# Recurrence scores below 32 tokens on four 32-column TensorE tiles, in a compact tile; sample values and decode states on such tiles too

## The chip, the cores and the metric

One core of one Trainium2 chip. The metric is the device time of one execution in microseconds. The kernel before took 1286.46 us, the median of 3 runs (1283.77 to 1287.47).

## The reference, cut to what matters

One layer of a decoder trunk over 1024 prompt tokens and 8 samples of 8 tokens each (together 1088 columns in the kernel): RMSNorm, one input projection, three groups of heads on its result, an output projection, then a gated ConvFFN. The group that the change touches most is the gated linear recurrence (HGRN2), 4 heads, key and value width 128:

```python
def step(S, blk):
    qc, kc, vc, gc = blk
    A = jnp.cumsum(gc, axis=2)
    decay = jnp.exp(jnp.where(mask, A[:, :, :, None, :] - A[:, :, None, :, :], -jnp.inf))
    scores = jnp.einsum("bhtd,bhsd,bhtsd->bhts", qc, kc, decay)
    o = jnp.einsum("bhts,bhsv->bhtv", scores, vc) + jnp.einsum("bhtd,bhdv->bhtv", qc * jnp.exp(A), S)
    A_end = A[:, :, -1:, :]
    S = jnp.exp(A_end[:, :, 0, :])[..., None] * S + jnp.einsum("bhsd,bhsv->bhdv", kc * jnp.exp(A_end - A), vc)
    return S, o
```

So the score of token t on an earlier token s is a product over 128 features, each with the decay between s and t. The samples go through the same with a state that is handed in. The change also touches the cross-attention of the samples (softmax of scores times 256 memory values per sample).

## The kernel before, in words

Features lie on partitions, tokens along the free side. The large products are split in two: weights and activations each into a high and a low part (fp32r), three matmuls (lines 283 to 285) for each block of 128 x 128 weights. The products of the heads are plain f32; the trace shows each such matmul as two passes, and each pass as a weight load (PEld) and a matmul (PE).

`hgrn(h)` is a generator, one for each head, with 20 steps. The scores between tokens are made level by level. Level b (1, 2, 4, ..., 64) makes the scores of the pairs that lie in the two halves of one stretch of 2b tokens: K of the first half times Q of the second. Between levels VectorE scales K and Q in place by products of forget gates (`T`, lines 725 to 727), so that after level b the decay over 2b tokens is in them. Before the levels come the scores of a token on itself (`dg`, line 670, and `dgs` for the samples, line 674). The 1024 tokens are 8 blocks of 128, and `scT` holds for each block a 128 x 128 matrix of scores (s on partitions, t along the free side); `scS` is the same for the 64 sample columns.

For the diagonal and the levels up to 16 (line 701) each block is one matmul with all 128 columns of K as weights and 128 (diagonal) or 64 (levels) columns of Q moving, though only the small squares near the diagonal are wanted; VectorE copies these out of PSUM into `scT` under a mask (`copy_predicated`, lines 671 and 703; 675 and 720 for the samples). Levels 32 and 64 (line 710) use the K columns of one half only, 32 or 64 weight columns, placed on the tile of TensorE that belongs to the output partitions, and ScalarE copies the result (line 714). Samples have levels 1, 2 and 4 (`scs`, line 718).

After the levels, K is transposed, the states S of the 8 blocks are made one after another, and `o` is scores times V plus S times Q (lines 767, 769). For the samples `os` is one matmul of the scores (line 773) and then one for each sample with its own state of 128 x 128 as weights and 8 columns of Q moving (line 775). Three chunks of normalisation follow.

`xattn()` is the cross-attention. For the samples, `ssc` (line 588) makes the scores of four samples on four 32-column tiles of TensorE, and `so` (line 608) multiplies 128 x 128 values by 16 columns of probabilities.

`weave` sets the order: the steps of `hgrn` and `xattn` are spread among the steps of the input projection that still has to be done (`WIN`, units of three chunks of 362 or 364 columns), so that projection matmuls stand between one level and the next. A planner in the framework then places instructions on each engine by their readiness, so the order on TensorE is near the written one and not quite it. `with tc.high_priority()` puts the evacuation of the projection first.

`msk` holds the masks and is loaded as f32 and converted once. `chist` holds the samples' conv history (128 x 352 f32); it is loaded at the start on ScalarE's queue and first read in the up projection of the FFN (`start_a`, line 1180). `enter("ou", ...)` begins the output stage; `out_rows` (line 882) issues the loads of the residual rows `xb` on SP's queue there.

Of the kernel before, what the change touches and what calls it, by code (L numbers as in the profile page):

```python
# [50 lines left out]
def trunk(ctx, tc, I, O):  # L51
# [30 lines left out]
    def hrow(name, cols=512, p=128, dt=F32):  # L82
        return now["wk"].tile([p, cols], dt, tag="half", name=name, bufs=HB)
# [70 lines left out]
    cst = const.tile([128, NC], F32, name="cst")  # L154
    msk = const.tile([128, 5 * 64 + 128], U8, name="msk")
    poolw = const.tile([128, 2, 128], F32, name="poolw")
    chist = const.tile([128, FT, 8, 2], F32, name="chist")

    def load_consts():
        nc.sync.dma_start(out=cst, in_=I["cst"])  # L160
        yield
        mskf = hrow("mskf", 5 * 64 + 128)
# [408 lines left out]
    def xattn():  # L571
# [88 lines left out]
    MD = 5 * 64  # L660

    def hgrn(h):
        f, K, Q, V = FR[h], KR[h], QR[h], VR[h]

        dm = msk[:, MD:MD + 128]
        for half in range(2):
            ps = bank(f"dg{h}{half}", [128, 4, 128])
            for i in range(4):
                n = 4 * half + i
                mm(ps[:, i, :], K[:, n * 128:n * 128 + 128], Q[:, n * 128:n * 128 + 128], start=True, stop=True)  # L670
            nc.vector.copy_predicated(out=scT[:, 4 * half:4 * half + 4, :],
                                      mask=dm.unsqueeze(1).to_broadcast([128, 4, 128]), data=ps)
        ps = bank(f"dgs{h}", [64, 64])
        mm(ps, K[:, NP:NT], Q[:, NP:NT], start=True, stop=True)
        nc.vector.copy_predicated(out=scS, mask=msk[0:64, MD:MD + 64], data=ps)
        tt(out=Q[:, 0:NT], in0=Q[:, 0:NT], in1=f[:, 0:NT], op=ALU.mult)
# [16 lines left out]
        for li, b in enumerate(LEVELS):  # L693
            w = NT if b <= 4 else NP
            nb = w // (2 * b)
            Qo = Q[:, 0:NP].rearrange("p (n j two r) -> p n j two r", n=8, two=2, r=b)[:, :, :, 1, :]
            o4 = scT.rearrange("p n (j two r) -> p n j two r", two=2, r=b)[:, :, :, 1, :]
# [17 lines left out]
            if b <= 4:  # L715
                pss = bank(f"scs{h}_{b}", [64, 32 // b, b])
                q = Q[:, NP:NT].rearrange("p (j two r) -> p j two r", two=2, r=b)[:, :, 1, :]
                mm(pss, K[:, NP:NT], q, start=True, stop=True)
                o = scS.rearrange("p (j two r) -> p j two r", two=2, r=b)[:, :, 1, :]
                nc.vector.copy_predicated(out=o, mask=msk[0:64, li * 64:li * 64 + 32].rearrange("p (j r) -> p j r", r=b), data=pss)  # L720
            Tb = f[:, 0:w] if b == 1 else T[:, TO[b]:TO[b] + w // b]
# [143 lines left out]

    enter("ou", 8, NQ, 6)
    order = [2, 3, 4, 5, 6, 7, 0, 1]
    x1d = tc.dram_tile([128, 8, NT], F32, name="x1d")
# [686 lines left out]
def layout(inp):  # L1555
# [26 lines left out]
    A["cst"] = cst  # L1582
    msk = np.zeros((128, 5 * 64 + 128), np.float32)
    for li, b in enumerate(LEVELS[:5]):
        for j in range(64 // b):
            msk[2 * j * b:2 * j * b + b, li * 64 + j * b:li * 64 + j * b + b] = 1
    msk[:, 320:448] = np.eye(128)
    A["msk"] = msk
# [52 lines left out]
```

## Time and profile before

| | us |
|---|---|
| median of 3 runs | 1286.46 |
| lowest, highest | 1283.77, 1287.47 |
| the profiled execution, its own time | 1288.27 |
| span of its trace | 1286.5 |
| PE busy | 1246.2 |
| DVE busy | 941.5 |
| ACT busy | 537.1 |
| POOL busy | 259.8 |
| granted clock of TensorE, mean | 0.984 of full |

The span is what the trace covers; the execution's own time is 1.8 us more. The recurrence runs from about 78 to 350 us of the span, woven with the input projection; the rest of the cross-attention and the pooling mixer follow to about 440, then output projection, up projection and down projection. PE is TensorE's matmuls, PEld its weight loads, DVE VectorE, ACT ScalarE, POOL GpSimd.

### The profile page before, as it was taken

How to read it: one execution, taken by the hardware profiler on the slowest of the kernel's cores; microseconds unless marked ns; L12 is line 12 of the kernel's file. 1: busy time of each engine (PE TensorE's matmuls, PEld its weight loads, DVE VectorE, ACT ScalarE, POOL GpSimd, SP SyncE). 2: the span in 40 equal slices, each digit the busy share in tenths (PEclk: the TensorE clock that was granted, in tenths of full speed). 3: DMA queues.
4: the chain of work that ended last, by engine and by line, in shares of the span. 5: the costliest groups of instructions: out<-in, count | busy, mean ns of one | idle time of the engine just before them, and what ended most of it. 6: DMA issues, size and time to landing. Idle time of an engine off the chain costs nothing.

```text
span 1286.5 us, 23500 instructions
## 1 busy us (share of the span) xinstructions
PE 1246.2 (97%) x9348; PEld 1206.1 (94%) x9348; DVE 941.5 (73%) x1672; ACT 537.1 (42%) x1015; POOL 259.8 (20%) x294
## 2 busy tenths in 40 slices
PE   6999999999999899989999999999999989999996
PEld 6999899998987799989999999999999989999996
DVE  7775767658496645988887789788876967967633
ACT  7732414122245445655333333333433425644542
POOL 0000000000010000234444544454322000100142
PEclk9999999999999898989999999999999999999998
DMA  8131011122201445322434543454312578344333
GB/s 260 35 115 50 34 50 33 50 63 93 85 24 39 144 137 175 105 67 91 137 133 145 183 142 132 142 183 134 93 58 75 194 253 290 94 124 150 97 93 105
DMA packets 75822, 148.11 MB, mean 115 GB/s; under 512 B 9136, under 2 KB 31280, under 8 KB 75712
## 3 DMA queue, kind: packets, MB, share of 16 engines
q1 hardware_dynamic: 71920, 141.77, 33.9%
q0 software_dynamic: 1280, 4.34, 0.9%
q8 instruction: 73, 1.20, 0.4%
q10 hardware_dynamic: 2512, 0.50, 0.2%
q14 instruction: 37, 0.30, 0.1%
HBM read 110.66 MB, written 35.93 MB: 114 GB/s over the span
## 4 chain that ended last, share of the span: by engine, by line
PE 82%; DVE 9%; ACT 3%; issue 3%; DMA 2%; DVEq 0%; POOL 0%; SPq 0%; ACTq 0%; POOLq 0%
PE sc L701 3%; PE po L926 2%; PE po L925 2%; PE uUa L1165 2%; PE uUa L1163 2%; PE po L924 2%; PE uUa L1164 2%; PE pV L1311 2%; PE pV L1313 2%; PE pV L1312 2%; PE pU L1311 2%; PE pU L1313 2%; PE pU L1312 2%; PE uPa L1164 2%; PE uPa L1165 2%
## 5 line engine op out<-in xcount | busy, mean ns | idle before, releaser
L1299 DVE TENSOR_TENSOR dlp<-drp,dhp 128x512 fp32r<-128x512 f32 x81 | 56.8, 712 | 39.6 <-ACT dhp L1298 38.6
L1298 ACT ACTIVATE dhp<-drp 128x512 fp32r<-128x512 f32 x81 | 49.6, 625 | 76.5 <-PE pP L1312 22.3
L1283 DVE TENSOR_TENSOR xop<-B,xop 128x544 fp32r<-128x544 f32 x70 | 50.2, 732 | 13.1 <-ACT xop L1304 13.0
L1304 ACT ACTIVATE xop<-B 128x544 fp32r<-128x544 f32 x70 | 44.3, 650 | 26.9 <-DVE xop L1283 13.0
L1313 PE MATMUL pP<-xop,dlp 128*128 128x272 f32 x176 | 51.2, 292 | 4.4 <-DVE dlp L1299 4.4
L1312 PE MATMUL pP<-xop,dhp 128*128 128x272 f32 x176 | 51.3, 292 | 0.0
L1311 PE MATMUL pP<-xop,dhp 128*128 128x272 f32 x176 | 51.3, 292 | 0.0
L1311 PE MATMUL pU<-xop,dhp 128*128 128x272 f32 x176 | 50.7, 288 | 0.1
L1311 PE MATMUL pV<-xop,dhp 128*128 128x272 f32 x176 | 50.7, 288 | 0.0
L1312 PE MATMUL pU<-xop,dhp 128*128 128x272 f32 x176 | 50.6, 288 | 0.0
L1312 PE MATMUL pV<-xop,dhp 128*128 128x272 f32 x176 | 50.6, 288 | 0.0
L1313 PE MATMUL pU<-xop,dlp 128*128 128x272 f32 x176 | 50.6, 287 | 0.0
L1313 PE MATMUL pV<-xop,dlp 128*128 128x272 f32 x176 | 50.6, 287 | 0.0
L1126 DVE TENSOR_TENSOR g<-g,uc 128x272 f32<-128x272 f32 x66 | 46.3, 702 | 0.8
L1099 POOL TENSOR_TENSOR us0a<-ura 128x512 f32<-128x512 f32 x11 | 19.2, 1749 | 121.5 <-DMA ura<-in_wup 103.8
L1193 DVE SCALAR_TENSOR_TENSOR g<-a,vec,g 128x1104 f32<-128x1104 f32 x22 | 31.7, 1443 | 14.6 <-ACT g L1191 14.6
L1196 ACT ACTIVATE g<-g 128x1104 f32<-128x1104 f32 x22 | 24.8, 1129 | 40.6 <-DVE g L1195 40.6
L1195 DVE SCALAR_TENSOR_TENSOR g<-a,vec,g 128x1104 f32<-128x1104 f32 x22 | 39.7, 1803 | 0.0
L214 ACT ACTIVATE whi<-raw 128x1024 fp32r<-128x1024 f32 (+1 forms) x24 | 24.5, 1022 | 35.9 <-PE pq L284 17.1
L701 PEld LDWEIGHTS sc<-Q,K 128*128 128x128 f32 x320 | 37.9, 192 | 1.3 <-issue 0.9
L701 PE MATMUL sc<-Q,K 128*128 128x64 f32 x320 | 38.4, 272 | 0.0
L1313 PEld LDWEIGHTS pP<-xop,dlp 128*128 128x128 f32 x176 | 33.7, 192 | 4.6 <-DVE dlp L1299 4.6
(2292 smaller groups left out, 5113.1 us busy)
## 6 DMA issues: line engine op xcount, KB each, us to landing
ds<-in_wdown SPq DMA_DIRECT2D x44, 256.0 KB, 3.1
ura<-in_wup SPq DMA_DIRECT2D x22, 512.0 KB, 4.2
urb<-in_wup SPq DMA_DIRECT2D x22, 512.0 KB, 3.7
sd<-ds SPq DMA_DIRECT2D x44, 256.0 KB, 2.0
drp<-sd SPq DMA_DIRECT2D x44, 256.0 KB, 2.7
fd<-g SPq DMA_DIRECT2D x20, 544.0 KB, 4.2
B<-fd SPq DMA_DIRECT2D x40, 272.0 KB, 5.3
drp<-in_wdown SPq DMA_DIRECT2D x37, 256.0 KB, 3.3
```

What stands on the lines that cost most here:

```text
L701: mm(ps[:, n, :, :], K[:, n * 128:n * 128 + 128], Qo[:, n], start=True, stop=True)
L1126: tt(out=dst, in0=dst, in1=s_, op=ALU.mult)
L1164: mm(ps, wh[:, w], xl[:, k], start=False, stop=False, skip_group_check=True)
L1165: mm(ps, wl[:, w], xh[:, k], start=False, stop=k == 3, skip_group_check=True)
L1195: stt(out=cw[:, 0:1104], in0=aw[:, 0:1104], scalar=col(V_CW, 3 * f), in1=cw[:, 0:1104], op0=ALU.mult, op1=ALU.add)
L1283: tt(out=out, in0=in0, in1=in1, op=ALU.subtract)
L1298: act(out=wh, in_=raw, func=AF.Copy)
L1299: tt(out=wl, in0=raw, in1=wh.bitcast(F32), op=ALU.subtract)
L1304: act(out=t[:, 0], in_=x, func=AF.Copy)
L1311: mm(ps, w[0][:, c], h, start=start, stop=False, skip_group_check=True)
L1312: mm(ps, w[0][:, c], l, start=False, stop=False, skip_group_check=True)
L1313: mm(ps, w[1][:, c], h, start=False, stop=stop, skip_group_check=True)
```

## The change

The diagonal and the levels 1 to 16 of the scores go through a new helper, `blocks`: a block of 128 tokens is four matmuls, each with 32 columns of K as weights on its own 32-column tile of TensorE (`tile_position=(0, 32 * j)`) and with the columns of Q that belong to those 32 tokens moving: 32 for the diagonal, 16 for a level. The result of a block is compact, 128 x 32 or 128 x 16. The scores are kept in a compact tile `scC` (128 partitions, 8 blocks and the samples, 32 columns), which lies in the memory of `chist`. The masks shrink to 16 columns a level and 32 for the diagonal. After level 16 ScalarE copies the four 32 x 32 squares of each block from `scC` to their places in `scT`, and two for the samples to `scS`. The sample values (`so`) and the decode states (`os`) are split in the same way into four 32-column tiles, with 16 and 8 moving columns. The load of `chist` moves from the start (ScalarE's queue) to the beginning of the output stage (SP's queue).

```diff
-    msk = const.tile([128, 5 * 64 + 128], U8, name="msk")
+    msk = const.tile([128, 112], U8, name="msk")
...
-    nc.scalar.dma_start(out=chist, in_=I["chist"])
...
-                    mm(so[:, ft, b, :], v_[:, t, ft * 128:ft * 128 + 128], spT[:, b // 4, t, o:o + 16],
-                       start=t == 0, stop=t == 1)
+                    for c in range(0, 128, 32):
+                        mm(so[c:c + 32, ft, b, :], v_[:, t, ft * 128 + c:ft * 128 + c + 32], spT[:, b // 4, t, o:o + 16],
+                           start=t == 0, stop=t == 1, tile_position=(0, c))
...
+    scC = chist.rearrange("p f b l -> p (f b l)")[:, 0:288].rearrange("p (n c) -> p n c", n=9)
+    nc.gpsimd.memset(scC, 0.0)
...
+    def blocks(ps, K, Q, at, cols, n=4):
+
+        for j in range(n):
+            mm(ps[32 * j:32 * j + 32, 0:cols], K[:, at + 32 * j:at + 32 * j + 32], Q(j), start=True, stop=True,
+               tile_position=(0, 32 * j))
...
-        dm = msk[:, MD:MD + 128]
-        for half in range(2):
-            ps = bank(f"dg{h}{half}", [128, 4, 128])
-            for i in range(4):
-                n = 4 * half + i
-                mm(ps[:, i, :], K[:, n * 128:n * 128 + 128], Q[:, n * 128:n * 128 + 128], start=True, stop=True)
-            nc.vector.copy_predicated(out=scT[:, 4 * half:4 * half + 4, :],
-                                      mask=dm.unsqueeze(1).to_broadcast([128, 4, 128]), data=ps)
...
+        dm = msk[:, MD:MD + 32]
+        ps = bank(f"dg{h}", [128, 8, 32])
+        for n in range(8):
+            blocks(ps[:, n], K, lambda j: Q[:, n * 128 + 32 * j:n * 128 + 32 * j + 32], n * 128, 32)
+        nc.vector.copy_predicated(out=scC[:, 0:8], mask=dm.unsqueeze(1).to_broadcast([128, 8, 32]), data=ps)
+        ps = bank(f"dgs{h}", [64, 32])
+        blocks(ps, K, lambda j: Q[:, NP + 32 * j:NP + 32 * j + 32], NP, 32, 2)
+        nc.vector.copy_predicated(out=scC[0:64, 8], mask=dm[0:64], data=ps)
...
             if b <= 16:
-                ps = bank(f"sc{h}_{b}", [128, 8, 64 // b, b])
+                g = 16 // b
+                ps = bank(f"sc{h}_{b}", [128, 8, 16])
                 for n in range(8):
-                    mm(ps[:, n, :, :], K[:, n * 128:n * 128 + 128], Qo[:, n], start=True, stop=True)
-                m4 = msk[:, li * 64:li * 64 + 64].rearrange("p (j r) -> p j r", r=b).unsqueeze(1)
-                nc.vector.copy_predicated(out=o4, mask=m4.to_broadcast([128, 8, 64 // b, b]), data=ps)
+                    blocks(ps[:, n], K, lambda j: Qo[:, n, g * j:g * j + g], n * 128, 16)
+                m4 = msk[:, li * 16:li * 16 + 16].rearrange("p (j r) -> p j r", r=b)
+                o4 = scC.rearrange("p n (j two r) -> p n j two r", two=2, r=b)[:, :, :, 1, :]
+                nc.vector.copy_predicated(out=o4[:, 0:8], mask=m4.unsqueeze(1).to_broadcast([128, 8, g, b]),
+                                          data=ps.rearrange("p n (j r) -> p n j r", r=b))
...
             if b <= 4:
-                pss = bank(f"scs{h}_{b}", [64, 32 // b, b])
+                pss = bank(f"scs{h}_{b}", [64, 16])
                 q = Q[:, NP:NT].rearrange("p (j two r) -> p j two r", two=2, r=b)[:, :, 1, :]
...
+                blocks(pss, K, lambda j: q[:, g * j:g * j + g], NP, 16, 2)
+                nc.vector.copy_predicated(out=o4[0:64, 8], mask=m4[0:64], data=pss.rearrange("p (j r) -> p j r", r=b))
+            if b == 16:
+                for j in range(4):
+                    c = slice(32 * j, 32 * j + 32)
+                    act(out=scT[c, :, c], in_=scC[c, 0:8], func=AF.Copy)
+                    if j < 2:
+                        act(out=scS[c, c], in_=scC[c, 8], func=AF.Copy)
...
-            mm(ps[:, b, :], s0[b // 4][:, b % 4, :], Q[:, NP + 8 * b:NP + 8 * b + 8], start=False, stop=True,
-               skip_group_check=True)
+            for c in range(0, 128, 32):
+                mm(ps[c:c + 32, b, :], s0[b // 4][:, b % 4, c:c + 32], Q[:, NP + 8 * b:NP + 8 * b + 8],
+                   start=False, stop=True, skip_group_check=True, tile_position=(0, c))
...
     enter("ou", 8, NQ, 6)
+    nc.sync.dma_start(out=chist, in_=I["chist"])
```

The host builds the smaller masks to match.

## Rows read from the trace of the kernel before

**Rows 1.** The page: busy time of each engine with its share of the span and instructions; gigabytes a second in 40 slices of the span; the chain that ended last by engine.

```profile
PE 1246.2 (97%) x9348; PEld 1206.1 (94%) x9348; DVE 941.5 (73%) x1672; ACT 537.1 (42%) x1015; POOL 259.8 (20%) x294
...
GB/s 260 35 115 50 34 50 33 50 63 93 85 24 39 144 137 175 105 67 91 137 133 145 183 142 132 142 183 134 93 58 75 194 253 290 94 124 150 97 93 105
...
PE 82%; DVE 9%; ACT 3%; issue 3%; DMA 2%; DVEq 0%; POOL 0%; SPq 0%; ACTq 0%; POOLq 0%
```

**Rows 2.** Windows of the recurrence, about one for each head: length, then the busy time of PE, PEld, DVE, ACT and POOL with their instructions, the granted clock, the DMA share and GB/s.

```profile
78.60:141.00 62.40, 62.40 (x451) 59.33 (x450) 37.41 (x72) 15.41 (x30) 1.25 (x2) 0.97 0.17 54
141.00:214.00 73.00, 73.00 (x505) 66.49 (x504) 55.36 (x112) 26.73 (x53) 1.08 (x2) 1.00 0.13 44
214.00:290.00 76.00, 76.00 (x528) 71.79 (x527) 49.87 (x98) 17.16 (x32) 4.40 (x8) 0.98 0.18 57
290.00:350.00 60.00, 60.00 (x474) 55.23 (x472) 38.92 (x79) 15.29 (x30) 1.23 (x4) 1.00 0.28 91
```

**Rows 3.** Lines with shapes kept apart, TensorE's matmuls of the score levels: weight tile, moving shape, count, busy us and mean ns of one.

```profile
L701 PE MATMUL sc<-Q,K 128*128 128x64 f32 x320 | 38.4, 272 | 0.0
...
L710 PE MATMUL sc<-Q,K 128*32 128x32 f32 x128 | 2.8, 197 | 0.0
```

**Rows 4.** Timeline of TensorE's matmuls around level 8 of head 0, no sample scores: start us, length us, engine, line, operation, tiles, shape and count.

```profile
108.43 0.33 PE L284 MATMUL pi<-h3l,whi 128*128 128x362 f32 x1
...
108.76 0.33 PE L283 MATMUL pi<-h4h,whi 128*128 128x362 f32 x1
108.92 1.89 PE L701 MATMUL sc<-Q,K 128*128 128x64 f32 x16
...
110.87 0.33 PE L285 MATMUL pi<-h4h,wlo 128*128 128x362 f32 x1
```

**Rows 5.** The same around level 1 of head 0, with its sample scores.

```profile
87.92 0.33 PE L285 MATMUL pq<-h3h,wlo 128*128 128x362 f32 x1
88.08 1.90 PE L701 MATMUL sc<-Q,K 128*128 128x64 f32 x16
89.91 0.30 PE L718 MATMUL scs<-Q,K 128*64 128x32 f32 x2
...
90.41 0.33 PE L284 MATMUL pq<-h4l,whi 128*128 128x362 f32 x1
```

**Rows 6.** The same around the diagonal of head 3 (two sample passes follow the 16).

```profile
288.56 0.33 PE L285 MATMUL pg<-h3h,wlo 128*128 128x364 f32 x1
288.73 1.95 PE L670 MATMUL dg<-Q,K 128*128 128x128 f32 x16
...
291.13 0.33 PE L284 MATMUL pg<-h4l,whi 128*128 128x364 f32 x1
```

**Rows 7.** The same around the decode states of head 1.

```profile
196.20 1.95 PE L775 MATMUL os<-Q,s 128*128 128x8 f32 x16
198.00 0.41 PE L283 MATMUL pf<-h2h,whi 128*128 128x362 f32 x1
```

**Rows 8.** The same around the values of one sample.

```profile
334.26 0.33 PE L283 MATMUL pu<-h1h,whi 128*128 128x364 f32 x1
334.43 0.96 PE L608 MATMUL so<-spT,svt 128*128 128x16 f32 x8
...
335.49 0.33 PE L285 MATMUL pu<-h1h,wlo 128*128 128x364 f32 x1
```

**Rows 9.** The same around level 32 of head 0, which is on two 32-column tiles.

```profile
112.68 0.32 PE L284 MATMUL pi<-h0l,whi 128*128 128x362 f32 x1
112.94 0.70 PE L710 MATMUL sc<-Q,K 128*32 128x32 f32 x32
...
113.83 0.33 PE L283 MATMUL pi<-h1h,whi 128*128 128x362 f32 x1
```

**Rows 10.** Timeline of TensorE: the cross-attention scores of four samples (four tiles), of one (one tile) and of two (two tiles), 256 moving columns each.

```profile
292.39 1.09 PE L588 MATMUL ssc<-skt,qs 128*32 128x256 f32 x16
...
296.27 1.05 PE L588 MATMUL ssc<-skt,qs 128*32 128x256 f32 x4
...
301.59 1.06 PE L588 MATMUL ssc<-skt,qs 128*32 128x256 f32 x8
```

**Rows 11.** Windows (columns as in rows 2) just after the decode states of heads 0 and 2, and the timeline of the first half of those of head 3.

```profile
132.30:135.70 3.40, 3.40 (x13) 3.40 (x13) 0.69 (x1) 0.22 (x1) 0.00 (x0) 0.50 0.00 0
272.20:275.70 3.50, 3.50 (x13) 3.50 (x13) 1.17 (x2) 0.16 (x1) 0.00 (x0) 0.51 0.00 0
...
343.29 0.95 PE L775 MATMUL os<-Q,s 128*128 128x8 f32 x8
```

**Rows 12.** Lines with shapes kept apart, VectorE's copies under a mask: shape, count, busy us and mean ns of one, idle time before them.

```profile
L703 DVE COPY_PREDICATED scT<-msk,sc 128x512 f32<-128x512 uint8 x20 | 19.1, 956 | 25.3 <-PE sc L701 25.2
L671 DVE COPY_PREDICATED scT<-msk,dg 128x512 f32<-128x512 uint8 x8 | 5.9, 732 | 0.1
L720 DVE COPY_PREDICATED scS<-msk,scs 64x32 f32<-64x32 uint8 x12 | 2.7, 225 | 0.0
```

**Rows 13.** One window (columns as in rows 2) at the join of head 0 and head 1.

```profile
144.00:150.00 6.00, 6.00 (x29) 4.06 (x28) 6.00 (x14) 2.96 (x8) 0.00 (x0) 1.00 0.24 87
```

**Rows 14.** Lines with shapes kept apart, ScalarE's copies of level 32.

```profile
L714 ACT ACTIVATE scT<-sc 32x256 f32<-32x256 f32 x8 | 3.0, 374 | 49.7 <-PE sc L710 49.7
```

**Rows 15.** Timeline of ScalarE's DMA queue at the start.

```profile
1.67 0.45 ACTq L168 DMA_DIRECT2D chist<-in_chist  x1
```

More of the change, by code (lines that the diff above doesn't have):

```diff
@@ L161, in load_consts @@
         yield
-        mskf = hrow("mskf", 5 * 64 + 128)
+        mskf = hrow("mskf", 112)
         nc.sync.dma_start(out=mskf, in_=I["msk"])
@@ L657, in trunk @@
     nc.gpsimd.memset(scS, 0.0)
+    scC = chist.rearrange("p f b l -> p (f b l)")[:, 0:288].rearrange("p (n c) -> p n c", n=9)
+    nc.gpsimd.memset(scC, 0.0)
     sout = hrow("sout").rearrange("p (h v) -> p h v", h=4)
     TO = {2: 0, 4: 544, 8: 816, 16: 952, 32: 1016, 64: 1048, 128: 1064}
-    MD = 5 * 64
+    MD = 80
+    def blocks(ps, K, Q, at, cols, n=4):
+        for j in range(n):
+            mm(ps[32 * j:32 * j + 32, 0:cols], K[:, at + 32 * j:at + 32 * j + 32], Q(j), start=True, stop=True,
+               tile_position=(0, 32 * j))
     def hgrn(h):
         f, K, Q, V = FR[h], KR[h], QR[h], VR[h]
-        dm = msk[:, MD:MD + 128]
-        for half in range(2):
-            ps = bank(f"dg{h}{half}", [128, 4, 128])
-            for i in range(4):
-                n = 4 * half + i
-                mm(ps[:, i, :], K[:, n * 128:n * 128 + 128], Q[:, n * 128:n * 128 + 128], start=True, stop=True)
-            nc.vector.copy_predicated(out=scT[:, 4 * half:4 * half + 4, :],
-                                      mask=dm.unsqueeze(1).to_broadcast([128, 4, 128]), data=ps)
-        ps = bank(f"dgs{h}", [64, 64])
-        mm(ps, K[:, NP:NT], Q[:, NP:NT], start=True, stop=True)
-        nc.vector.copy_predicated(out=scS, mask=msk[0:64, MD:MD + 64], data=ps)
+        dm = msk[:, MD:MD + 32]
[6 more added lines that the diff above has]
+        nc.vector.copy_predicated(out=scC[0:64, 8], mask=dm[0:64], data=ps)
         tt(out=Q[:, 0:NT], in0=Q[:, 0:NT], in1=f[:, 0:NT], op=ALU.mult)
@@ L696, in hgrn @@
             Qo = Q[:, 0:NP].rearrange("p (n j two r) -> p n j two r", n=8, two=2, r=b)[:, :, :, 1, :]
-            o4 = scT.rearrange("p n (j two r) -> p n j two r", two=2, r=b)[:, :, :, 1, :]
             if b <= 16:
-                ps = bank(f"sc{h}_{b}", [128, 8, 64 // b, b])
+                g = 16 // b
+                ps = bank(f"sc{h}_{b}", [128, 8, 16])
                 for n in range(8):
-                    mm(ps[:, n, :, :], K[:, n * 128:n * 128 + 128], Qo[:, n], start=True, stop=True)
-                m4 = msk[:, li * 64:li * 64 + 64].rearrange("p (j r) -> p j r", r=b).unsqueeze(1)
-                nc.vector.copy_predicated(out=o4, mask=m4.to_broadcast([128, 8, 64 // b, b]), data=ps)
+                    blocks(ps[:, n], K, lambda j: Qo[:, n, g * j:g * j + g], n * 128, 16)
[3 more added lines that the diff above has]
+                                          data=ps.rearrange("p n (j r) -> p n j r", r=b))
             else:
@@ L715, in hgrn @@
             if b <= 4:
-                pss = bank(f"scs{h}_{b}", [64, 32 // b, b])
+                pss = bank(f"scs{h}_{b}", [64, 16])
                 q = Q[:, NP:NT].rearrange("p (j two r) -> p j two r", two=2, r=b)[:, :, 1, :]
-                mm(pss, K[:, NP:NT], q, start=True, stop=True)
-                o = scS.rearrange("p (j two r) -> p j two r", two=2, r=b)[:, :, 1, :]
-                nc.vector.copy_predicated(out=o, mask=msk[0:64, li * 64:li * 64 + 32].rearrange("p (j r) -> p j r", r=b), data=pss)
+                blocks(pss, K, lambda j: q[:, g * j:g * j + g], NP, 16, 2)
[6 more added lines that the diff above has]
+                        act(out=scS[c, c], in_=scC[c, 8], func=AF.Copy)
             Tb = f[:, 0:w] if b == 1 else T[:, TO[b]:TO[b] + w // b]
@@ L1582, in layout @@
     A["cst"] = cst
-    msk = np.zeros((128, 5 * 64 + 128), np.float32)
+    msk = np.zeros((128, 112), np.float32)
     for li, b in enumerate(LEVELS[:5]):
-        for j in range(64 // b):
-            msk[2 * j * b:2 * j * b + b, li * 64 + j * b:li * 64 + j * b + b] = 1
-    msk[:, 320:448] = np.eye(128)
+        for p in range(128):
+            if p % (2 * b) < b:
+                j = p % 32 // (2 * b)
+                msk[p, li * 16 + j * b:li * 16 + j * b + b] = 1
+    for p in range(128):
+        msk[p, 80 + p % 32] = 1
     A["msk"] = msk
```

## The prediction

> **What bounds the kernel now.** I read the page first: in the busy totals and the chain of waits the reader is to see that TensorE carries the end, busy 1246.2 of 1286.5 us and 82% of the chain, VectorE 9% [rows 1]. The change sits in the recurrence, so I then read that stage by windows. In 78.6 to 350 us TensorE is busy 100% of every window, VectorE 60 to 76%, ScalarE 23 to 37% [rows 2]. The lines view gives the price of what is replaced: the scores below 32 tokens are 320 passes and 38.4 us, about 120 ns a pass [rows 3]. (An f32 matmul stands in the trace as two passes, each with its own weight load: 8 blocks x 5 levels x 4 heads = 160 matmuls, 320 passes.) Last I read the timeline of single groups, since what counts is not an instruction's length but how long the projection's matmuls are held up.
>
> **How a group is priced.** Projection matmuls start 0.165 us apart (108.43 to 108.76, two steps) [rows 4]. A group between them costs the time from the start of the one before to the start of the second one after, less two steps (0.33). A level without sample scores: 110.87 - 108.76 - 0.33 = 1.78 us [rows 4]. A level with them: 90.41 - 87.92 - 0.33 = 2.16 [rows 5]. Diagonal with its sample part: 291.13 - 288.56 - 0.33 = 2.24 [rows 6]. The 16 passes of decode states: 198.00 - 196.20 = 1.80 [rows 7]. A sample's values: 335.49 - 334.26 - 0.33 = 0.90 [rows 8].
>
> These passes have 128, 64, 16 or 8 moving columns, yet all take 100 to 120 ns (38.4 us / 320 with 64 columns [rows 3], 1.80 / 16 with 8 [rows 7]). So the moving columns don't set the pace; the load of 128 weight columns does, as far as these rows tell. That load is what the change divides.
>
> **The new price.** The kernel already has such a group: the 32-token level runs 16 matmuls (32 passes) on two 32-column tiles, and costs 113.83 - 112.68 - 0.33 = 0.82 us, of which the burst is 0.50, from its first start to its last (0.70 [rows 9] less the 0.20 of the last pass [rows 3]); so 32 ns a pass on one tile (16 passes each), and about 0.32 us is for going into the narrow form and back. The new groups put 64 passes on four tiles, again 16 on each. Whether four tiles run as freely as two is shown by the sample scores of the cross-attention: 16 passes on four tiles last 1.09 us, 8 passes on two 1.06, 4 passes on one 1.05 [rows 10]. Tiles overlap almost wholly, so I price a new group by passes per tile: 0.82 us. Sample scores add one more short block on two tiles, 2 x 32 ns: 0.89.
>
> The Trainium skill ("TensorEngine Tiling (Array Packing)", Performance Considerations, Instruction Overhead) speaks against this: it gives each matmul some 60 cycles whatever its columns and advises against taking a tiling factor from a dimension that is already small, and here the moving side is 16 or 8. By that, if the cost is paid in one line, 64 passes at 25 ns (an estimate: 60 cycles at 2.4 GHz) are 1.6 us and the gain is gone; it is a rival below. The trace of before disagrees as far as it goes: 32 passes in 0.50 us are under 16 ns each [rows 9].
>
> **The change part by part, four heads.**
> Levels 1, 2, 4: 12 groups x (2.16 - 0.89) = 15.2 us.
> Levels 8, 16: 8 x (1.78 - 0.82) = 7.7.
> Diagonal: 4 x (2.24 - 0.89) = 5.4; with 32 moving columns it is the shape of [rows 9] itself.
> Decode states: the burst of 1.80 becomes 0.50 plus about 0.1 to load the next full weights plus 0.1 to go into the narrow form = 0.7; 4 x 1.1 = 4.3.
> Sample values: 8 groups, 8 passes per tile: 0.32 + 0.25 = 0.57 for 0.90; 8 x 0.33 = 2.6.
> Together 35.2 us off TensorE, all on the path in a stage where TensorE never rests.
>
> Clock: twice, after the decode states of heads 0 and 2, the granted clock falls to 0.50 for 3.4 us [rows 11], the 1.2 GHz level. TensorE had just run 16 passes of 8 moving columns. Head 3, whose 16 passes stand in two halves of 0.95 us, has no fall behind the first [rows 11], and the new burst is shorter than such a half. I take both falls as gone: half of 3.4, twice = 3.2 (own bounds: 0 gained, or as many new ones lost).
>
> VectorE: 28 predicated copies of 512 columns (19.1 + 5.9 = 25 us) become 4 of 256 and 20 of 128. Unseen in that form; between 0.22 us (the 64x32 copy) and 0.73 (the 512) [rows 12], nearer the small one for 128: about 0.27, and 0.4 for 256. That is 25 - 5.4 - 1.6 = 18 us less, 4.5 a head, beside TensorE. It matters at the joins between heads, where VectorE is busy 6 of 6 us [rows 13]: there TensorE saves 1.35 on the diagonal and VectorE only 2 x 0.73 - 0.4 = 1.06 ahead of the product of Q. I give back 0.3 x 3 joins, 1 us.
>
> ScalarE gets six copies a head from the compact tile into scT and scS, at most 6 x 0.37 = 2.2 us by the 32x256 copy [rows 14]. Their reader, the `o` matmuls, stands two levels later, so they cost nothing by themselves; what is queued behind them is the evacuation of the next projection (sigmoid, then VectorE, then the bank). Cover is ScalarE's idle two thirds. Bounds 0 to 8.8 us; I take 1.
>
> DMA: the load of chist leaves ScalarE's queue at 1.67 us [rows 15] and goes to SP's queue at the output stage, ahead of the four xb loads and the weights behind them. It waits for the last ScalarE copy of head 3, which is out of the way a stage earlier, and its reader is in the FFN. One more issue of 0.45 us: nothing, or 0.45 if exposed. At the start 176 KB less is moved, and the mask is smaller: between 0 and 0.7 us (176 KB at the 260 GB/s of that slice [rows 1]); I take 0, as TensorE's start hangs on ScalarE too. The memset of the compact tile is on GpSimd, which is nearly idle [rows 2].
>
> Sum: 35.2 + 3.2 - 1 - 1 = 36.4. The profiled execution took 1288.27 us, 1.8 above the median of the runs, so 1251.9 there and 1250.1 against the median.
>
> **The rivals.**
> (a) Four tiles don't run as freely as two. That they do is seen for passes of 256 columns [rows 10]; for short ones the 0.50 us of level 32 [rows 9] may be an issue pace, 32 passes at 16 ns, and not the tiles'. Then 64 passes take 1.0: groups cost 1.33 and 1.39, savings are 12 x 0.77 + 8 x 0.45 + 4 x 0.85 + 4 x 0.6 + 8 x 0.08 = 19, and the time is 1250 + 16 = 1266. Chance 0.12. For it: the same number fits both readings. Against: four tiles end within the time of one [rows 10].
> (b) VectorE's chain becomes the bound: each level's scores must be copied and K and Q scaled before the next level. TensorE then gets back only what VectorE saves, 18 us: 1286.5 - 18 = 1268. For it: 6 of 6 us at the joins [rows 13]. Against: 60 to 76% in the stages as a whole [rows 2], and the chain per level shortens by the copy. Chance 0.12.
> (c) Slower: passes on different tiles stand in one line. Place: every new group; price 32 ns a pass (the pace of one tile [rows 9]): 64 passes are 2.0 us, groups 2.34 and 2.47, so +0.56 x 8, +0.31 x 12, +0.23 x 4, states +0.43 x 4, sample values +0.43 x 8 = +14, time 1301. It decides from about 25 ns a pass, where a group (64 x 0.025 + 0.32 = 1.9) costs what it costs now. Against: the overlap of tiles [rows 9, 10]. Chance 0.06.
> (d) The line at a lower price, at break-even: no change, 1284 to 1288. Chance 0.04. By the skill's 25 ns the estimate is 1286.
>
> **How the numbers follow.** Forecast 0.66, own range 1243 to 1259 (clock falls -3 to +3, ScalarE up to 8.8, start 0.7, unseen copies). The range is widened upward to 1269 to take in (a) and (b); what is left out is (c), (d) and the ends. Downward 1242. A measurement of this kernel tells about 0.3%, 4 us. Faster by more than that: 0.66 + 0.12 + 0.12 = 0.90; within: 0.04; slower: 0.06.
>
> **What would show it.** In the changed profile: score passes four times as many, bursts of 0.5 us for 64 passes with projection matmuls held up 0.8 to 0.9 us; 1.3 would be (a), over 2 would be (c). TensorE's idle time before score groups stays under 1 us a head; if it grows and is put down to VectorE, (b). No fall of the clock behind the decode states, and none new behind scores. The evacuations' waits on ScalarE unchanged. Stages after 430 us as long as before. I am wrong if short passes on four tiles don't overlap, or if the time taken off TensorE comes back as waits.

## The result, and the profile after

The changed kernel takes 1245.51 us, the median of 4 runs (1240.97 to 1246.40), against 1286.97 (1283.77 to 1289.69) for the kernel before beside it: a ratio of 0.9672 [0.9639, 0.9705]. That is 41.5 us less where 36.4 were forecast; the forecast of 1250.1 is 4.6 us above the median and the range held it. From profiled execution to profiled execution it is 1288.27 to 1246.40, 41.9 us.

The page of the changed kernel, busy totals and chain by engine, beside [rows 1]:

```profile
PE 1204.8 (97%) x10916; PEld 1161.0 (93%) x10916; DVE 927.3 (75%) x1668; ACT 545.1 (44%) x1039; POOL 259.3 (21%) x295
...
PE 82%; DVE 11%; issue 3%; ACT 3%; DMA 2%; SPq 0%; DVEq 0%; POOL 0%; ACTq 0%; POOLq 0%
```

TensorE still carries the end with the same share of the chain, and is busy 41.4 us less, nearly the whole of what the kernel gained. So what came off TensorE came off the end, and nothing new stands in its place.

The first product of the output projection tells in which part of the kernel that was. The view of one tile, `po`, first for the kernel after:

```profile
L940 PE MATMUL po<-c,ow000h x8: 286/410/428, 399.5 to 404.1; 128*128 128x272 f32 x8
```

and for the kernel before:

```profile
L924 PE MATMUL po<-c,ow000h x8: 288/428/593, 441.2 to 446.5; 128*128 128x272 f32 x8
```

The output projection starts at 399.5 instead of 441.2 us, 41.7 earlier; the same view of the down projection's `pP` gives 989.7 instead of 1031.0. All of the gain lies ahead of the output stage, where the change was made. From there to the end the kernel takes 845.1 us, and took 845.2 before.

Lines with shapes kept apart of the kernel after, TensorE's score levels, then VectorE's masked copies; columns as in [rows 3] and [rows 12]:

```profile
L669 PE MATMUL sc<-Q,K 128*32 128x16 f32 x1280 | 14.8, 185 | 0.0
...
L711 DVE COPY_PREDICATED chist<-msk,sc 128x128 f32<-128x128 uint8 x20 | 7.1, 354 | 5.4 <-PE sc L669 3.0 <-PE scs L669 1.9
...
L679 DVE COPY_PREDICATED chist<-msk,dg 128x256 f32<-128x256 uint8 x4 | 1.8, 442 | 0.4 <-PE dgs L669 0.4
```

1280 passes take 14.8 us of TensorE, where 320 took 38.4 [rows 3]. One pass is still 185 ns long, against 272: the gain is not in a shorter pass but in how many are under way at once. The masked copies of the recurrence's prompt tokens take 7.1 + 1.8 = 8.9 us, for 25.0 [rows 12], 16 less for the 18 forecast.

What counts is how long the projection is held up, so the groups are read on the timeline of TensorE's matmuls (columns as in [rows 4]): level 1 of head 0 with its sample scores, level 8 of head 0, the diagonal of head 1, the decode states of head 1, those of head 3 and what follows them, and the values of one sample, all of the kernel after:

```profile
86.22 0.33 PE L284 MATMUL pq<-h3h,wlo 128*128 128x362 f32 x1
86.47 0.71 PE L669 MATMUL sc<-Q,K 128*32 128x16 f32 x62
...
87.01 0.19 PE L669 MATMUL scs<-Q,K 128*32 128x16 f32 x1
...
87.03 0.18 PE L669 MATMUL sc<-Q,K 128*32 128x16 f32 x1
...
87.45 0.33 PE L283 MATMUL pq<-h4l,whi 128*128 128x362 f32 x1
...
95.24 0.33 PE L283 MATMUL pi<-h0l,whi 128*128 128x364 f32 x1
95.50 0.74 PE L669 MATMUL sc<-Q,K 128*32 128x16 f32 x64
...
96.44 0.33 PE L282 MATMUL pi<-h1h,whi 128*128 128x364 f32 x1
...
138.52 0.73 PE L669 MATMUL dg<-Q,K 128*32 128x32 f32 x62
...
139.52 0.33 PE L284 MATMUL pq<-h0h,wlo 128*128 128x362 f32 x1
...
178.59 0.72 PE L790 MATMUL os<-Q,s 128*32 128x8 f32 x64
179.24 0.43 PE L282 MATMUL pf<-h2h,whi 128*128 128x362 f32 x1
...
302.89 0.32 PE L790 MATMUL os<-Q,s 128*32 128x8 f32 x17
...
304.16 0.88 PE L801 MATMUL oss<-osq,cst 128*128 128x364 f32 x2
304.97 0.45 PE L608 MATMUL so<-spT,svt 128*32 128x16 f32 x32
...
305.61 0.33 PE L282 MATMUL pg<-h5h,whi 128*128 128x362 f32 x1
```

By the rule of the prediction (start to start of the second one after, less 0.33) level 8 costs 96.44 - 95.24 - 0.33 = 0.87 us for 1.78 [rows 4], level 1 87.45 - 86.22 - 0.33 = 0.90 for 2.16 [rows 5]. The states hold up the next matmul 179.24 - 178.59 = 0.65 us for 1.80 [rows 7]. The diagonal and the values here don't stand behind a projection matmul, so I add the way in that level 8 shows, 95.50 - 95.24 = 0.26: the diagonal is 0.26 + 1.00 (138.52 to 139.52) - 0.33 = 0.93 for 2.24 [rows 6], a sample's values 0.26 + 0.64 (304.97 to 305.61) - 0.33 = 0.57 for 0.90 [rows 8]. The states of head 3 run as one burst with the values of two samples, 302.89 to 304.16, with one way in and out; that is 1.27 us where 0.65 + 2 x 0.57 would be 1.79.

Windows of the kernel after, columns as in [rows 2]: one for each head, the join of heads 0 and 1 ahead of them, and one in the down projection that an experiment needs:

```profile
137.00:143.00 6.00, 6.00 (x97) 4.57 (x96) 6.00 (x14) 2.65 (x6) 1.08 (x2) 1.00 0.12 45
...
77.50:132.00 54.50, 54.50 (x808) 50.88 (x808) 35.16 (x74) 18.65 (x38) 1.25 (x2) 1.00 0.19 63
132.00:188.00 56.00, 56.00 (x806) 50.59 (x805) 42.73 (x92) 23.21 (x49) 1.08 (x2) 1.00 0.14 49
188.00:254.00 66.00, 66.00 (x869) 61.06 (x869) 45.79 (x97) 20.76 (x43) 3.13 (x5) 1.00 0.18 61
254.00:306.00 52.00, 51.99 (x1024) 43.17 (x1023) 40.44 (x90) 18.23 (x41) 2.51 (x7) 1.00 0.38 117
...
990.00:1000.00 10.00, 5.53 (x34) 5.32 (x33) 9.16 (x16) 3.45 (x7) 0.55 (x1) 0.83 0.64 220
```

TensorE is busy all of the time in each head, VectorE now up to 78% (40.44 of 52), and the granted clock is full throughout: the two falls of [rows 11] are gone. At the join VectorE is busy 6 of 6 us as before [rows 13], and TensorE as well.

### The profile page after: what moved, and what is told of

It reads as the page before. It is cut to its first block, busy times and chain, and to the rows that moved or that the text cites. A ratio compares the mean times of both kernels' runs of the same rounds, so it can differ in the third digit from the quotient of the medians.

```text
span 1244.6 us, 26679 instructions
## 1 busy us (share of the span) xinstructions
PE 1204.8 (97%) x10916; PEld 1161.0 (93%) x10916; DVE 927.3 (75%) x1668; ACT 545.1 (44%) x1039; POOL 259.3 (21%) x295
## 3 DMA queue, kind: packets, MB, share of 16 engines
q0 software_dynamic: 1280, 4.34, 0.9%
## 4 chain that ended last, share of the span: by engine, by line
PE 82%; DVE 11%; issue 3%; ACT 3%; DMA 2%; SPq 0%; DVEq 0%; POOL 0%; ACTq 0%; POOLq 0%
PE po L942 2%; PE po L941 2%; PE uUa L1181 2%; PE po L940 2%; PE uUa L1179 2%; PE uUa L1180 2%; PE pV L1327 2%; PE pV L1328 2%; PE pV L1329 2%; PE pU L1327 2%; PE pU L1328 2%; PE pU L1329 2%; PE uPa L1180 2%; PE uPa L1181 2%; PE uPa L1179 2%
## 5 line engine op out<-in xcount | busy, mean ns | idle before, releaser
L1212 ACT ACTIVATE g<-g 128x1104 f32<-128x1104 f32 x22 | 24.8, 1129 | 41.9 <-DVE g L1211 41.9
L1215 DVE TENSOR_TENSOR g<-g,ra 128x560 f32<-128x560 f32 x22 | 36.9, 1678 | 0.0
L1328 PEld LDWEIGHTS pP<-xop,dhp 128*128 128x128 f32 x176 | 33.7, 191 | 0.0
```

The lines of the kernel that those rows point to most:

```text
L1328: mm(ps, w[0][:, c], l, start=False, stop=False, skip_group_check=True)
```

## The experiments

**Theory A**, that of the prediction: a group is priced by the passes on its busiest 32-column tile, some 32 ns each, because passes on different tiles overlap; the time saved lies on the end because TensorE never rests there. **Theory B**: the gain comes from VectorE's smaller copies. **Theory C**: a pace of issue, or of the whole array, sets the price, and the widths don't matter. The kernels ran in three groups, each beside the kernel before: order of the tiles, 64-column tiles and more moving columns beside 1291.29 us; sample parts undone, more and less work for VectorE and level 64 beside 1289.56; the sample parts alone, two and four blocks and chist at both places beside 1287.85. Sums are held against the 1245.51 of the changed kernel, which was measured in a group of its own.

**Order of the tiles.** The same 64 passes, first all blocks on tile 0, then on tile 1, and so on:

```diff
-                for n in range(8):
-                    blocks(ps[:, n], K, lambda j: Qo[:, n, g * j:g * j + g], n * 128, 16)
+                for j in range(4):
+                    c = slice(32 * j, 32 * j + 32)
+                    for n in range(8):
+                        mm(ps[c, n], K[:, n * 128 + 32 * j:n * 128 + 32 * j + 32], Qo[:, n, g * j:g * j + g],
+                           start=True, stop=True, tile_position=(0, 32 * j))
```

Expected:

> Same matmuls for the levels 1 to 16, but all eight blocks of one 32-column tile stand in the program before the next tile's. Theory A (tiles work side by side only where the queue holds matmuls of several tiles close together): 64 passes at 32 ns go nearly in one line, a level group costs about 2.3 us in place of 0.88, 20 groups make +20 to +30 us, time 1266 to 1276 us. Theory B (a group costs its passes per tile, whatever the order): 1245.5 us, groups still 0.88. Everything else is as in the changed kernel.

Measured: 1269.32 us, ratio 0.9822 [0.9768, 0.9876]. The timeline of TensorE around level 8 of head 0:

```profile
99.75 0.33 PE L283 MATMUL pi<-h0l,whi 128*128 128x364 f32 x1
100.01 1.90 PE L710 MATMUL sc<-Q,K 128*32 128x16 f32 x64
...
102.11 0.33 PE L282 MATMUL pi<-h1h,whi 128*128 128x364 f32 x1
```

The group costs 102.11 - 99.75 - 0.33 = 2.03 us for 0.87. 20 groups x 1.16 = 23.2 more than 1245.51 is 1268.7, and 1269.32 was measured. This is rival (c) brought about by order alone: with the tiles one after another the narrow form of a level without sample scores costs more than the full one (1.78 [rows 4]). Count, widths and work of the passes are unchanged, so a fixed price per pass (theory C) falls.

**64-column tiles.** Two tiles of 64 instead of four of 32, so half the passes and half of the scores left out (of each 64 columns of K one half meets the wrong Q):

```diff
-                    blocks(ps[:, n], K, lambda j: Qo[:, n, g * j:g * j + g], n * 128, 16)
+                    for j in range(2):
+                        c = slice(64 * j, 64 * j + 64)
+                        mm(ps[c, n], K[:, n * 128 + 64 * j:n * 128 + 64 * j + 64], Qo[:, n, 2 * g * j:2 * g * j + g],
+                           start=True, stop=True, tile_position=(0, 64 * j))
```

Expected:

> Levels 1 to 16 as two matmuls of 64 weight columns a block in place of four of 32, 16 columns moving, so half the passes, each with twice the weight columns. The Q columns of the second 32 tokens of each pair are left out, so these scores are not the reference's; VectorE's copies are unchanged. Theory A (a pass lasts as long as the load of its weight columns, tiles side by side): 16 passes of 61 ns on each of two tiles, burst 0.98 us, group 1.3, +8.5 us, time 1254. Theory B (the number of passes counts, a line at some 9 ns a pass as the changed kernel's 64 in 0.55 us would also allow): burst 0.28, group 0.6, time 1240.

Measured: 1254.91 us, ratio 0.9716 [0.9652, 0.978]. The timeline as above:

```profile
96.38 0.33 PE L283 MATMUL pi<-h0l,whi 128*128 128x364 f32 x1
96.64 1.11 PE L710 MATMUL sc<-Q,K 128*64 128x16 f32 x32
...
97.96 0.33 PE L282 MATMUL pi<-h1h,whi 128*128 128x364 f32 x1
```

Half as many passes cost more: 97.96 - 96.38 - 0.33 = 1.25 us, 0.38 more. Level 1 of head 0, whose sample scores stay on 32-column tiles, costs 87.56 - 85.81 - 0.33 = 1.42, 0.52 more. 8 x 0.38 + 12 x 0.52 = 9.3, and 9.4 was measured. The weight columns set the price, not the number of passes; rival (a), a pace of 16 ns a pass whatever the tile, would have made this group shorter.

**More moving columns, 32 and 64.** All 32 tokens of a tile move instead of the 16 wanted, or 64 (where the copy takes the first 32, so every second tile's scores are those of other tokens). The edit of the matmuls, without that of the copy:

```diff
-                    blocks(ps[:, n], K, lambda j: Qo[:, n, g * j:g * j + g], n * 128, 16)
+                    blocks(ps[:, n], K, lambda j: Q[:, n * 128 + 32 * j:n * 128 + 32 * j + 32], n * 128, 32)
```

and for 64 columns

```diff
+                    blocks(ps[:, n], K, lambda j: Q[:, n * 128 + 64 * (j // 2):n * 128 + 64 * (j // 2) + 64], n * 128, 64)
```

Expected, for 32 and then for 64:

> Levels 1 to 16 with all 32 columns of Q of a tile moving in place of the 16 that are wanted; the copy takes the wanted half. Theory A (weight load sets the pace up to 32 moving columns, as for the diagonal): groups 0.88 to 0.92, time within 1 us of 1245.5. Theory B (moving columns set the pace): burst 0.55 becomes 1.1, +0.55 x 20 = +11 us, time 1256.

> Levels 1 to 16 with 64 columns of Q moving on each tile (the 64 around it); the copy takes the first 32 of them, so for every second tile the scores are of other tokens than the reference's. Theory A (the longer of weight load and moving columns, tiles side by side): 64 columns of f32 last about 54 ns a pass (61 ns a pass at level 64, which has both 64), 16 a tile, burst 0.87 to 0.98, group 1.2 to 1.3, +6.5 to +8.5 us, time 1252 to 1254. Theory B (a pass costs the same whatever moves): 1246.

Measured with 32: 1245.30 us, ratio 0.9636 [0.9582, 0.969]; with 64: 1251.18, ratio 0.968 [0.9627, 0.9733]. The timeline of level 8 with 32 columns:

```profile
95.70 0.76 PE L669 MATMUL sc<-Q,K 128*32 128x32 f32 x64
```

and with 64:

```profile
95.32 0.32 PE L284 MATMUL pq<-h7h,wlo 128*128 128x362 f32 x1
95.57 1.10 PE L669 MATMUL sc<-Q,K 128*32 128x64 f32 x64
...
96.87 0.33 PE L283 MATMUL pi<-h0l,whi 128*128 128x364 f32 x1
```

Twice the columns are nearly free: bursts of 0.76 for 0.74 us, and no difference in time. Four times the columns cost 96.87 - 95.32 - 0.33 = 1.22 us a group, 0.35 more (20 x 0.35 = 7.0, and 5.7 was measured): 0.35 / 16 passes on a tile = 22 ns a pass, from 32 to some 54. That fits a pass that lasts as long as the longer of its weight load and its moving columns: up to 32 columns the load of 32 weight columns, at 64 the moving ones.

**Sample parts undone.** Sample values and decode states as one full-width matmul again, the scores as changed:

```diff
-                    for c in range(0, 128, 32):
-                        mm(so[c:c + 32, ft, b, :], v_[:, t, ft * 128 + c:ft * 128 + c + 32], spT[:, b // 4, t, o:o + 16],
-                           start=t == 0, stop=t == 1, tile_position=(0, c))
+                    mm(so[:, ft, b, :], v_[:, t, ft * 128:ft * 128 + 128], spT[:, b // 4, t, o:o + 16],
+                       start=t == 0, stop=t == 1)
...
-            for c in range(0, 128, 32):
-                mm(ps[c:c + 32, b, :], s0[b // 4][:, b % 4, c:c + 32], Q[:, NP + 8 * b:NP + 8 * b + 8],
-                   start=False, stop=True, skip_group_check=True, tile_position=(0, c))
+            mm(ps[:, b, :], s0[b // 4][:, b % 4, :], Q[:, NP + 8 * b:NP + 8 * b + 8], start=False, stop=True,
+               skip_group_check=True)
```

Expected:

> The changed kernel with decode states and sample values back on the full 128 columns. Theory A (they are worth their TensorE time, and the clock fell because of the decode states): +4.3 (states) + 2.6 to 3.6 (values), and the two falls of the clock behind the states of some heads come back, up to +3.2: time 1252 to 1256. Theory B (the falls went for another reason): no fall to 0.5 between 100 and 350 us, time 1252.

Measured: 1262.78 us, ratio 0.9794 [0.9762, 0.9825], 17.3 above the changed kernel and more than expected. Windows just behind the decode states of heads 1 and 2, and over the sample values:

```profile
181.20:184.60 3.40, 3.40 (x13) 3.40 (x13) 0.69 (x1) 0.22 (x1) 0.00 (x0) 0.50 0.00 0
249.50:252.90 3.40, 3.40 (x12) 3.40 (x13) 1.23 (x2) 0.22 (x1) 0.00 (x0) 0.50 0.00 0
...
314.30:324.50 10.20, 10.20 (x42) 10.20 (x42) 3.89 (x7) 3.34 (x8) 0.00 (x0) 0.50 0.18 52
```

The falls of the clock to 1.2 GHz are back, and longer: 3.4 + 3.4 + 10.2 = 17.0 us at half, which costs 8.5. The groups' own price is 4 x 1.15 (states) + 8 x 0.33 (values) = 7.2; together 15.7 of the 17.3; from the first diagonal to the last projection matmul the two traces differ by 15.6. Ahead of each fall TensorE had run the 16 full-width passes with 8 moving columns; here the values of the samples, 8 full-width passes with 16 columns each, follow those of head 3 closely, and the fall lasts over them.

**The sample parts alone**, added to the kernel before (the same edit the other way round). Expected:

> The kernel before with sample values and decode states alone on 32-column tiles, scores as before. Theory A: -4.5 (states) -3.7 (values), and the two falls of the clock behind the states gone, -3.2: time 1275. Theory B (the falls come from something else in the stage, such as the full-width scores): falls to 0.5 between 100 and 350 us stay, time 1278.

Measured: 1277.22 us, ratio 0.9909 [0.988, 0.9939], 10.6 less than the kernel before beside it. One window over its recurrence:

```profile
79.00:340.00 261.00, 260.99 (x2337) 240.74 (x2335) 181.51 (x357) 74.54 (x145) 7.96 (x16) 1.00 0.19 63
```

The clock is full throughout, with the score groups still as before. So the falls go with the states and values and not with the scores; 7.2 for the groups and 3.4 for the two falls [rows 11] make 10.6.

**More work for VectorE.** A copy of 512 columns under a mask of zeros after each level, which changes no score:

```diff
+                nc.vector.copy_predicated(out=scT[:, 0:4, :], mask=none.unsqueeze(1).to_broadcast([128, 4, 128]),
+                                          data=ps.rearrange("p n c -> p (n c)").unsqueeze(1).to_broadcast([128, 4, 128]))
```

Expected:

> The changed kernel with one more masked copy of 128x512 on VectorE behind each level's copy (the mask is zero, so nothing is written), in the chain before K and Q are scaled: 20 x 0.72 = 14.4 us more of VectorE, TensorE as in the changed kernel. Theory A (TensorE is the bound, VectorE has room): +0 to +4 us, time 1246 to 1250. Theory B (the gain came through VectorE's shorter chain): +14 us, time 1260.

Measured: 1246.45 us, ratio 0.9664 [0.9632, 0.9696]. The line of the added copies:

```profile
L715 DVE COPY_PREDICATED scT<-none,sc 128x512 f32<-128x512 uint8 x20 | 14.9, 746 | 0.0
```

14.9 us more on VectorE, nearly what the change had taken off it, cost nothing that the medians show. In its one trace the stretch from the first diagonal (77.4) to the output projection (402.1) is 3.5 us longer than that of the changed kernel, and the stages behind it are shorter (840.0 us for 845.1) at a higher clock; so up to 3.5 of the 14.9 may be paid there.

**Less work for VectorE, nothing else.** The kernel before with its copies cut to a quarter, three quarters of the scores left out:

```diff
-                nc.vector.copy_predicated(out=o4, mask=m4.to_broadcast([128, 8, 64 // b, b]), data=ps)
+                nc.vector.copy_predicated(out=o4[:, 0:2], mask=m4.to_broadcast([128, 2, 64 // b, b]), data=ps[:, 0:2])
```

(the diagonal likewise). Expected:

> The kernel before, with VectorE's masked copies cut to a quarter of their columns (128x128 for the levels and for each half of the diagonal), so the scores of three quarters of the blocks are left out; TensorE does all it did. VectorE is relieved of about 15 us. Theory A: 0 to -3 us against the kernel before, time 1283 to 1287. Theory B: -15 us, time 1272.

Measured: 1288.14 us, ratio 0.9991 [0.9969, 1.0013]. Its line for the copies, beside [rows 12]:

```profile
L703 DVE COPY_PREDICATED scT<-msk,sc 128x128 f32<-128x128 uint8 x20 | 7.1, 355 | 26.3 <-PE sc L701 26.3
```

The copies take 7.1 us as in the changed kernel (there 354 ns each, here 355), VectorE waits for TensorE instead, and the time stands still. Theory B falls from both sides, as the cause of more than a few us.

This run shows something else. Its TensorE program is that of the kernel before, and yet its clock falls at other places and for longer. Windows just behind the decode states of heads 0 and 1, and from those of head 3 over the sample values:

```profile
135.60:139.00 3.40, 3.40 (x12) 2.85 (x10) 0.62 (x2) 0.00 (x0) 0.00 (x0) 0.51 0.02 5
200.40:203.80 3.40, 3.40 (x13) 3.40 (x12) 0.53 (x1) 0.06 (x1) 0.00 (x0) 0.50 0.00 0
343.80:354.00 10.20, 10.20 (x38) 9.65 (x39) 3.29 (x7) 1.38 (x5) 0.00 (x0) 0.50 0.15 12
```

That is 17.0 us at half, as in the run with the sample parts undone, for 6.9 in the kernel before [rows 11]. So the long falls there are not a matter of the narrow scores.

**Level 64 on two 32-column tiles too**, a try for a better version:

```diff
-                    for j in range(nj):
-                        s0 = 2 * j * b
-                        mm(ps[s0:s0 + b, n, :], K[:, n * 128 + s0:n * 128 + s0 + b], Qo[:, n, j, :],
-                           start=True, stop=True)
+                    for s0 in (0, 64) if b == 32 else (0, 32):
+                        j = s0 // (2 * b)
+                        mm(ps[s0:s0 + 32, n, :], K[:, n * 128 + s0:n * 128 + s0 + 32], Qo[:, n, j, :],
+                           start=True, stop=True, tile_position=(0, s0))
```

Expected:

> The changed kernel with level 64 also on 32-column tiles: its 64 weight columns as two loads of 32 on two tiles, 32 passes in place of 16. Theory A: burst 0.92 becomes 16 x 54 to 61 ns or less (64 columns move, so they and not the load set the pace; a group of two narrow tiles costs the same as one wide tile): 0 to -0.4 us a head, time 1244 to 1246. Theory B (the load of weight columns alone sets the pace): burst 0.5, -0.42 x 4 = -1.7 us, time 1243.8. Told apart by the burst in the trace, not by the time.

Measured: 1249.64 us, ratio 0.9692 [0.966, 0.9724]; its interval overlaps that of the changed kernel. The burst of a level lasts 1.09 us where it lasted 1.15, in keeping with 64 moving columns setting the pace at either width. The output projection starts at 399.2 us and the first diagonal at 77.0, 322.2 apart, where the changed kernel has 321.3: no gain ahead of it. From there to the end it is 847.9 us for 845.1, in stages that the edit doesn't touch. A window of the down projection, to be held against the last of the windows above:

```profile
990.00:1000.00 10.00, 5.54 (x29) 5.32 (x28) 8.91 (x16) 3.18 (x6) 0.55 (x1) 0.66 0.61 207
```

The same work at a granted clock of 0.66 instead of 0.83. Why the clock falls longer there in one kernel than in the other isn't settled.

**Two and four blocks in a row on each tile**, between the interleaved order and the order of the first experiment:

```diff
-                for n in range(8):
-                    blocks(ps[:, n], K, lambda j: Qo[:, n, g * j:g * j + g], n * 128, 16)
+                for n0 in range(0, 8, 2):
+                    for j in range(4):
+                        c = slice(32 * j, 32 * j + 32)
+                        for n in range(n0, n0 + 2):
+                            mm(ps[c, n], K[:, n * 128 + 32 * j:n * 128 + 32 * j + 32], Qo[:, n, g * j:g * j + g],
+                               start=True, stop=True, tile_position=(0, 32 * j))
```

(4 for 2 in the other). Expected, for two and then for four:

> The changed kernel, levels 1 to 16 with the matmuls of two blocks (4 passes) on one 32-column tile in a row before the next tile's. In the run with eight blocks in a row a tile's last three or four passes stood beside the next tile's first, no more. Theory A (each tile takes some four passes in advance, and the stream behind waits once a tile is full): 4 passes still fit, burst 0.50 to 0.60 us as with one block, time 1245 to 1247. Theory B (any run of passes on one tile beyond the two of one matmul goes in line): 64 passes, about half in line, burst 1.0 us, +9 us, time 1254.

> The same with four blocks (8 passes) in a row. Theory A: of each 8 passes some four go alone and the rest beside the next tile's, burst 1.1 to 1.4 us, group 1.4 to 1.7, +11 to +17 us, time 1256 to 1262. Theory B: as with eight blocks, burst 1.7, 1269.

Measured with two: 1245.67 us, ratio 0.9661 [0.9635, 0.9686]; with four: 1259.3 in one run. The timeline of level 8 with two:

```profile
94.30 0.33 PE L283 MATMUL pi<-h0l,whi 128*128 128x364 f32 x1
94.56 0.83 PE L711 MATMUL sc<-Q,K 128*32 128x16 f32 x64
...
95.59 0.33 PE L282 MATMUL pi<-h1h,whi 128*128 128x364 f32 x1
```

and with four:

```profile
97.50 0.33 PE L283 MATMUL pi<-h0l,whi 128*128 128x364 f32 x1
97.76 1.50 PE L711 MATMUL sc<-Q,K 128*32 128x16 f32 x64
...
99.46 0.33 PE L282 MATMUL pi<-h1h,whi 128*128 128x364 f32 x1
```

Groups of 0.96 and 1.63 us, between 0.87 and 2.03. Four passes in a row on one tile (two blocks) still overlap with the next tile's, eight mostly don't. 20 x 0.76 = 15.2 for four blocks agrees with the 13.8 measured.

**The load of chist at both places**, at the start on ScalarE's queue again and in the output stage:

```diff
     nc.scalar.dma_start(out=poolw, in_=I["poolw"])
+    nc.scalar.dma_start(out=chist, in_=I["chist"])
```

Expected:

> The changed kernel with the conv history loaded at the start too, on ScalarE's queue as before, besides the load at the output stage. Theory A: the 0.5 us by which the recurrence starts earlier than before (diagonal of head 0 at 78.2 for 78.7) is this load; it starts at 78.7 again, time +0.5. Theory B: the load hides behind others, diagonal at 78.2, no change.

Measured: 1246.93 us in one run, within the spread of the changed kernel; its first `dg` starts at 78.4 us where that of the changed kernel starts at 78.2. Without any change to the start, the first `dg` of the other kernels with this change stands between 77.0 and 79.4. What the load costs at the start can't be told from the scatter and stays open. That the compact tile keeps its own place, with chist loaded at the start alone, was not tried.

## Why the prediction held

**The price of a group** was the step on which all rested, and it held: 0.87 and 0.90 us for 0.82 and 0.89. With the measured prices, the sum by its own terms is 12 x 1.26 = 15.1 for levels 1 to 4 (forecast 15.2), 8 x 0.91 = 7.3 for levels 8 and 16 (7.7), 4 x 1.31 = 5.2 for the diagonal (5.4), 4 x 1.15 = 4.6 for the states (4.3) and 8 x 0.33 = 2.6 for the sample values (2.6). Together 34.8, forecast 35.2. (Two of the prediction's products are written short: 4 x 1.1 for the states is 4.4, and half of 3.4 us twice is 3.4 and not 3.2.)

The reason given for it held too, with one thing that the prediction didn't say: it took the overlap of tiles from [rows 9, 10] without asking in which order the passes came. Written tile by tile, the same passes cost 2.03 us. The Trainium skill ("TensorEngine Tiling (Array Packing)", Performance Considerations, Instruction Overhead) was weighed there: some 60 cycles for each matmul, by the prediction's reading paid in one line. The runs disagree with that reading: 64 passes started within 0.74 - 0.185 = 0.55 us, under 9 ns each, which for two passes a matmul is still under 18, against 25 by the estimate there.

**The clock**: both falls behind the decode states are gone, 3.4 us as forecast at 3.2, and the sample parts alone take them away. What the prediction missed is how much the falls can take: 17.0 us at half, 8.5 lost, in the run with the sample parts undone and in the one with less work for VectorE. So with the states and values at full width the clock took 3.4 us in one trace and 8.5 in two, and the mean clock of other executions of the kernel before ranges from 0.975 to 0.989; that the forecast's 3.2 fits may in part be luck. What decides how long the falls last is not shown.

**VectorE**: the copies gave 16 us for 18, since 0.354 and 0.442 us were longer than the 0.27 and 0.4 guessed. The size was off and nothing hung on it: the 1 us given back at the joins was not paid. The run with 14.9 us more on VectorE shows the room, so a VectorE busy 6 of 6 us at the join isn't a VectorE that sets the end. Of the waits ahead of TensorE's weight loads in 78 to 306 us, those of the diagonals for VectorE are these, 1.6 us where they were 1.5:

```profile
PEld dg L669 <- DVE oy L252: 0.8, 1, 0.8
PEld dg L669 <- DVE oy L258: 0.8, 1, 0.8
```

**ScalarE**: 1 us was given back for its extra copies, and no part of the trace shows it paid. The copies themselves take 8.4 us of ScalarE (16 of 414 ns into `scT`, 8 of 227 into `scS`), close to the upper bound of 8.8, beside a TensorE that doesn't wait for them.

**What is left.** 34.8 + 3.4 = 38.2 of the 41.7 us by which the output projection starts earlier. The forecast gave back 2 us that weren't paid; the other 3.5 us weren't in it. The burst that the states of head 3 share with two samples' values is 0.5 of them. Another 0.5 is the start of the recurrence (first diagonal at 78.2 for 78.7), which scatters by more than that. The largest part, 1.8, is TensorE's pause ahead of the output projection, ended by ScalarE's copy of the first weights: the timeline of `po`, before and then after, with the idle time ahead of it in brackets:

```profile
441.24 0.59 PE L924 MATMUL po<-c,ow000h 128*128 128x272 f32 x1 [5.45 <-ACT ow000h L895]
...
399.53 0.39 PE L940 MATMUL po<-c,ow000h 128*128 128x272 f32 x1 [3.64 <-ACT ow000h L911]
```

From the last projection matmul to `po` it is 4.0 us in the changed kernel and 5.8 before, but 5.3 in the run with 64-column tiles, which differs from the changed kernel in nothing near it, and 4.6 with the sample parts alone, so this is no effect of the change that can be counted on. The last 0.7 us were not traced to a place.

**The rivals.** (a) and (c) need passes on different tiles to queue in one line; they did so only where the order put a tile's passes together. (b), VectorE's chain, was refuted from both sides, a few us excepted. (d), break-even, would have needed the 1.9 us per group that four blocks in a row come near to (1.63).

## What to carry to other kernels

A short matmul whose result is mostly thrown away is priced by its weight columns, so cut those; price what comes out by the passes on the busiest tile, each at the longer of its weight load and its moving columns, and add some 0.3 us for each entry into the narrow form and back. Write such passes so that the tile changes at least every few of them: in tile order the same work lost about as much (23.2 us) as the change had gained in the levels up to 16 (15.1 + 7.3 = 22.4). Look at the granted clock behind bursts of full-width loads with few moving columns, since what they cost may stand in the matmuls after them.

## What the runs showed of the hardware

The order of passes in the program sets how far tiles overlap: 0.87, 0.96, 1.63 and 2.03 us for the same 64 passes with 2, 4, 8 and 16 passes in a row on one tile. That fits a tile that takes a handful of passes in advance and stops those behind it when it is full; the runs show the times, and the queue is argued from them. In keeping with it, the sample passes of level 1, which are written later, start among the last of the score passes (one at 87.01 us, with a score pass behind it at 87.03).

A burst of 16 full-width passes with 8 moving columns is followed by 3.4 us at half the clock in some heads and not in others: heads 0 and 2 in the kernel before, 1 and 2 with the sample parts undone, 0 and 1 with less work for VectorE. In the last two the clock is also at half for 10.2 us behind head 3's, over the sample values. The 64 narrow passes that do the same work were followed by none, in the changed kernel and in each of the ten other runs that have them. Why one burst is followed by a fall and the next is not stays open.

Between kernels with the same code in the later stages, the traces take from 840.0 us (more work for VectorE, mean clock 0.990) to 847.9 us (level 64, 0.985) from the output projection to the end. That is as much as the uncertainty of a comparison, so a small difference is better read from the stage that was changed.
